# A block's down-projection by seven block products of eight, with the weight sums made by accumulating transfers

## The chip, the cores and the metric

The kernel runs on one core of a Trainium2 chip, in one launch. The metric is the device time of the execution in microseconds. Five engines work beside each other, each with its own queue in order: PE (TensorE), DVE (VectorE), ACT (ScalarE), POOL (GpSimd) and SP (SyncE, which here only issues transfers).

## What is computed

One decoder block for 2048 tokens of width 1024, in float32: a retention group and an attention group (8 heads each) side by side, an output projection, and a gated convolutional MLP. The change concerns the MLP, and the attention beside which it puts new work:

```python
def conv_ffn(h, w_up, conv_w, conv_b, w_down):
    S = h.shape[1]
    u = jnp.einsum('bsd,df->bsf', h, w_up)
    up = jnp.pad(u, ((0, 0), (CONV_WIDTH - 1, 0), (0, 0)))
    u = conv_b + sum(conv_w[j] * up[:, j:j + S] for j in range(CONV_WIDTH))
    gate, val = u[..., :D_FF], u[..., D_FF:]
    return jnp.einsum('bsf,fd->bsd', jax.nn.silu(gate) * val, w_down)
...
        x = x + conv_ffn(rms_norm(x, ffn_norm_w[l]), w_up[l], conv_w[l], conv_b[l], w_down[l])
    return rms_norm(x, final_norm_w)
```

D_FF is 2816, 22 blocks of 128.

## The kernel before

Every float32 product is made of three products of rounded parts: an operand is split into a high part (by ACT, L65) and the rest, called lo (by POOL or DVE, L69), and `mm3` (L71 to L75) multiplies high by high, high by lo and lo by high into one PSUM bank. So a split of 128x512 is one ACT and one POOL or DVE operation, and three matmuls of 128x128 by 128x512 make one block product.

The stages follow each other: the input projection to about 225 us; then retention (`ret_stream`) and attention (`att_stream`, L567), whose steps `side_by_side` (L482) mixes, and attention beside the first half of the output projection, to 1390 us; then for each half of 1024 tokens the forms of its tokens (`half_0_forms`, `half_1_forms`), the up-projection `up` (L1125) and the down-projection `down` (L1209). A scheduler sets the order of each engine from the order in which these streams issue their steps. In attention POOL adds up denominators (`den`, L793) from ACT's exponentials (`pc`, L782), and splits q and k as they are loaded; SP loads q, k, kpe and v (L718 to L734) and stores denominators (`den_s`, L807) and outputs in one queue.

`up` already multiplies 2x2 blocks with seven products in place of eight (Strassen-Winograd): per block fb of 128 features 7 x 12 matmuls. The sums of weight blocks that this needs are made by POOL in `weight_forms` (L1091): per fb four additions or subtractions (L1095, L1108) and seven lo splits, a step of it at each product (`next(prep)` in `product`, L1138). DVE adds the products into u (L1147), does the convolution (L1153, L1154, 128x1024, with ACT's L1152) and the gate (L1178, L1179); g goes to `g_s` in DRAM.

`down` goes through two quarters q of four token tiles, for each through 22 blocks fb; a step has 4 x 2 x 3 = 24 matmuls into eight banks, so that it needs all of PSUM from its first step. Its g split's lo is DVE's, the two weight splits' lo POOL's; the loads (512 KB of weights, 256 KB of g) go two steps ahead. At the end of a quarter come the residual (`finish`, L1220), squares (L1226), `rstd` and the scaling (L1228 to L1231), and the stores, which `pay` (L915) issues.

Of the kernel before, what the change touches and what calls it, by code (L numbers as in the profile page):

```python
# [29 lines left out]
NFB = DFF // P  # L30
EPS = 1e-6
# [23 lines left out]
class Block:  # L55
# [511 lines left out]
    def att_stream(self):  # L567
# [11 lines left out]
        self.at, mx, owed = 0, maxima(), 0.0  # L579
        for n, (h, g) in enumerate(groups):  # L580
# [412 lines left out]
    def half_0_forms(self):  # L993
# [10 lines left out]
        for i in range(4):  # L1004
# [3 lines left out]
            if i == 0:  # L1008
                self.up_load(0)
# [16 lines left out]
    def z1_load(self, n, r=None):  # L1026
        t = Z1_ORDER[n]
        r = (self.raws[n % 2] if r is None else r).rearrange("p (a k x) -> p a k x", a=2, k=4)
        self.att_load(t, r, self.p1.rearrange("p (k x) -> p k x", k=4), self.ms[n % 2].rearrange("p (a k x) -> p a k x", a=2, k=4))

    def z1_early(self, n):

        if n == 2 * NFB - 3:
            self.nc.sync.dma_start(self.u2.rearrange("p a b -> p (a b)"), self.a["ffn_norm_w"].broadcast_to([P, D]))
            self.ms = self.slots(1)
        if n >= 2 * NFB - 2:
            k = n - (2 * NFB - 2)
            self.z1_load(k, self.u.rearrange("p a b -> p (a b)")[:, k * D:(k + 1) * D])

    def half_1_forms(self):  # L1040
# [5 lines left out]
        for n, t in enumerate(Z1_ORDER):  # L1046
# [14 lines left out]
            if n == 1:  # L1061
                self.up_load(0)
# [19 lines left out]
    def all_forms(self, half):  # L1082
# [5 lines left out]
        for n in range(2):  # L1088
            yield from self.down_prepare(n)

    def weight_forms(self):  # L1091

        nc, a = self.nc, self.a
        t1, t2 = (self.fs[0][:, k * 512:(k + 1) * 512] for k in range(2))
        sub = lambda o, x, y: nc.gpsimd.tensor_tensor(o, x, y, op=ALU.subtract)  # L1095
        W = self.W = {}

        def raw(fb, j, k):
            return self.raws[(2 * fb + j + 2) % 4][:, k * 512:(k + 1) * 512]

        def put(fb, n, src):
            W[fb, n] = self.slot_split(src, P)
        for fb in range(NFB):
            self.up_load(fb + 1)
            g0, g1, v0, v1 = (raw(fb, j, k) for j in range(2) for k in range(2))
            put(fb, 0, g0)
            yield
            nc.gpsimd.tensor_tensor(t1, v0, v1, op=ALU.add)  # L1108
            sub(t2, t1, g0)
            put(fb, 1, t2)  # L1110
            yield
            sub(v0, g0, v0)
            put(fb, 6, v0)
            yield
            put(fb, 4, t1)
# [298 lines left out]
```

## Time and profile before

| what | value |
|---|---|
| median of 3 runs (lowest, highest) | 2917.74 us (2916.3, 2919.93) |
| the profiled execution's own time | 2915.82 us |
| its span, first to last instruction | 2914.0 us |
| mean granted TensorE clock | 0.976 of full speed |
| matmuls | 12672 |
| moved by the DMA engines | 332.85 MB, all issued by SP but 2.4 MB of instructions |

Busy times are those of one profiled execution. A line such as L69 can be a helper's, so groups are told apart by the tile that they write (w, F, k, den). "Idle before, <-releaser" is the time in which an engine stood still ahead of these instructions and what let it go on. A stretch gives each engine's busy time with the number of its instructions.

### The profile page before, as it was taken

The numbers are of one execution on the slowest core, as the hardware profiler recorded it, in microseconds if no ns is written. First come the engines' busy times: TensorE is split into PE (matmuls) and PEld (weight loads), VectorE is DVE, ScalarE is ACT, GpSimd is POOL, SyncE is SP. The second block draws the span as 40 slices with busy tenths as digits, with TensorE's granted clock in tenths as the row PEclk, the third lists the DMA queues.
The fourth block names the chain that finished last, engine by engine and source line by source line (L and its number), as shares of the span: only waits on it lengthen the run. The fifth ranks groups of instructions, "written<-read, shape, count | busy, mean of one in ns | idle before, by whom it ended". The sixth has DMA issues, their size and how long they took to land.

```text
span 2914.0 us, 37511 instructions
## 1 busy us (share of the span) xinstructions
PE 2726.3 (94%) x12672; PEld 2217.6 (76%) x12672; DVE 1932.9 (66%) x3349; ACT 1353.5 (46%) x2588; POOL 1976.0 (68%) x1480
## 2 busy tenths in 40 slices
PE   7998999998999999989999999899986999999998
PEld 6976777776777777767788887688874888887887
DVE  8756766767776776844468888834165888886243
ACT  5435566566665565651333343334334443333243
POOL 2035665666655565664699999776568999995564
PEclk9999999999999999989999999999997999999999
DMA  7663122222211121335722222375462222225453
GB/s 262 225 206 93 45 66 69 66 77 83 80 53 61 54 66 44 95 109 200 249 71 87 83 69 87 101 235 178 155 205 73 87 82 71 87 72 174 145 198 106
DMA packets 153506, 332.85 MB, mean 114 GB/s; under 512 B 35033, under 2 KB 68569, under 8 KB 147169
## 3 DMA queue, kind: packets, MB, share of 16 engines
q1 hardware_dynamic: 153312, 330.45, 35.3%
q8 instruction: 100, 1.64, 0.2%
q14 instruction: 94, 0.76, 0.1%
HBM read 237.64 MB, written 92.75 MB: 113 GB/s over the span
## 4 chain that ended last, share of the span: by engine, by line
PE 54%; DVE 3%; POOL 3%; DMA 2%; ACT 1%; issue 1%; SPq 0%; POOLq 0%; ACTq 0%; DVEq 0%
PE b L75 16%; PE b L74 16%; PE b L73 16%; DMA raw<-mixa_s 1%; PE x L677 1%; PE pm L74 1%; PE pm L75 1%; PE pm L73 1%; POOL w L69 1%; POOL F L69 0%; POOL m L69 0%; PE sm L743 0%; PE u L75 0%; PE s L775 0%; DVE w L1154 0%
## 5 line engine op out<-in xcount | busy, mean ns | idle before, releaser
L69 POOL TENSOR_TENSOR w<-raw,w 128x512 fp32r<-128x512 f32 (+2 forms) x315 | 519.7, 1667 | 243.5 <-ACT w L65 233.7
L74 PE MATMUL b<-F,w 128*128 128x512 f32 x1232 | 486.6, 395 | 6.6 <-POOL F L69 6.6
L75 PE MATMUL b<-F,w 128*128 128x512 f32 x1232 | 492.1, 399 | 0.0
L73 PE MATMUL b<-F,w 128*128 128x512 f32 x1232 | 485.3, 394 | 0.0
L793 POOL TENSOR_TENSOR den<-den,pc 128x512 f32<-128x512 f32 (+2 forms) x256 | 294.9, 1152 | 231.7 <-ACT pc L782 213.5
L65 ACT ACTIVATE w<-raw 128x512 fp32r<-128x512 f32 (+2 forms) x328 | 214.6, 658 | 336.6 <-PE b L75 191.6
L73 PE MATMUL b<-w 128*128 128x512 f32 x832 | 329.1, 396 | 19.6 <-DVE u L1147 11.3
L74 PE MATMUL b<-w 128*128 128x512 f32 x832 | 327.4, 393 | 0.0
L75 PE MATMUL b<-w 128*128 128x512 f32 x832 | 326.8, 393 | 0.0
L69 DVE TENSOR_TENSOR w<-xr,w 128x512 fp32r<-128x512 f32 x88 | 112.1, 1274 | 287.8 <-ACT w L65 287.8
L74 PEld LDWEIGHTS b<-F,w 128*128 128x128 f32 x1232 | 232.1, 188 | 66.9 <-POOL F L69 7.1
L73 PEld LDWEIGHTS b<-F,w 128*128 128x128 f32 x1232 | 232.1, 188 | 56.7 <-DVE u L1147 1.5
L75 PEld LDWEIGHTS b<-F,w 128*128 128x128 f32 x1232 | 232.0, 188 | 53.7
L784 DVE TENSOR_TENSOR pc<-s,pc 128x512 fp32r<-128x512 f32 (+1 forms) x320 | 197.2, 618 | 95.3 <-ACT s L783 74.8
L782 ACT ACTIVATE pc<-s 128x512 fp32r<-128x512 f32 (+1 forms) x320 | 173.2, 541 | 176.8 <-PE s L780 172.4
L1153 DVE SCALAR_TENSOR_TENSOR w<-u,cw,w 128x1024 f32<-128x1024 f32 x88 | 163.9, 1863 | 127.5 <-ACT w L1152 127.5
L1152 ACT ACTIVATE w<-u,cw 128x1024 f32<-128x1024 f32 x88 | 109.5, 1244 | 271.1 <-DVE u L1147 234.3
L73 PE MATMUL pm<-w,h 128*128 128x512 f32 x512 | 209.3, 409 | 11.4 <-DVE r_g L126 3.8
L74 PE MATMUL pm<-w,h 128*128 128x512 f32 x512 | 203.6, 398 | 0.0
L69 POOL TENSOR_TENSOR w<-xr,w 128x512 fp32r<-128x512 f32 x110 | 200.9, 1843 | 3.4 <-ACT w L65 3.4
L75 PE MATMUL pm<-w,h 128*128 128x512 f32 x512 | 203.1, 397 | 0.0
L73 PEld LDWEIGHTS b<-w 128*128 128x128 f32 x832 | 158.2, 190 | 56.5 <-DVE u L1147 15.0
(271 smaller groups left out, 6608.9 us busy)
## 6 DMA issues: line engine op xcount, KB each, us to landing
raw<-in_w_down SPq DMA_DIRECT2D x88, 512.0 KB
h<-hT_s SPq DMA_DIRECT2D x32, 1024.0 KB
xr<-in_w_up SPq DMA_DIRECT2D x44, 512.0 KB
raw<-in_w_up SPq DMA_DIRECT2D x44, 512.0 KB
g_s<-w SPq DMA_DIRECT2D x44, 512.0 KB
xr<-g_s SPq DMA_DIRECT2D x88, 256.0 KB
hT_s<-hT SPq DMA_DIRECT2D x16, 1024.0 KB
raw<-in_w_ret SPq DMA_DIRECT2D x16, 512.0 KB
```

The lines of the kernel that those rows point to most:

```text
L65: nc.scalar.activation(hi, src, AF.Copy)
L69: eng.tensor_tensor(lo, src, f32(hi), op=ALU.subtract)
L73: mm(out, lhsT=lh, rhs=rh, start=start, stop=False)
L74: mm(out, lhsT=lh, rhs=rl, start=False, stop=False)
L75: mm(out, lhsT=ll, rhs=rh, start=False, stop=stop)
L677: mm(ps[:, x * P:x * P + 256], lhsT=l, rhs=r, start=n == 0, stop=n == len(ops) - 1)
L782: nc.scalar.activation(pc[:, 0, r0:], ps[:, r0:], AF.Exp, scale=ATT_SCALE)
L784: nc.vector.tensor_tensor(pc[:, 1, r0:], ps[:, r0:], f32(pc[:, 0, r0:]), op=ALU.subtract)
L793: nc.gpsimd.tensor_tensor(den[:, r0:], den[:, r0:], hi[:, r0:], op=ALU.add)
L1152: nc.scalar.activation(acc, x[:, 2:1026], AF.Identity, scale=w2, bias=b)
L1153: nc.vector.scalar_tensor_tensor(acc, x[:, 1:1025], w1, acc, op0=ALU.mult, op1=ALU.add)
```

## The change

The down-projection of a half becomes one 2x2 block product with seven products: the token halves (512 tokens) and halves of the 2816 features on one side, the halves of features and of output columns on the other. Each product p has 11 blocks of 128 features, so there are 77 steps (`ND`), each with 4 x 3 = 12 matmuls into four banks, one per token tile. The g rows lie in a tile G (22 x 512 KB), loaded by `row(k)` in the steps listed; G takes the place of the up-projection's tile F. DVE makes the sums of the token side (`sums(i)`, 44 operations of 128x512 in steps 6 to 49) and adds each product to the four result blocks it belongs to (`meet`: for the first ACT makes four copies per token tile, for the other six DVE makes 1, 2, 2, 3, 1 and 1 additions per tile, 40 in all). A step's two splits have their lo on DVE (POOL for the first three). The closing of the rows is spread over the last steps; the half's last steps do one eviction, one square and a closing per tile.

The sums of weight blocks, four for the up-projection (22 blocks of 256 KB each) and four for the down-projection (11 blocks each), are made in DRAM during attention: one operand is copied by a DRAM-to-DRAM transfer from SP, and the other is added by an accumulating transfer from POOL. `att_stream` asks for one transfer at every third step of `att_group`, 60 copies and 60 accumulating ones in all (512 KB each for up, 768 or 512 KB for down). `weight_forms` then only loads the seven forms of an fb (1.79 MB in place of 1 MB) and splits them. The weights lie in DRAM in blocks that fit this. Some signs change in `up`.

```diff
@@ att_stream, after L586 @@
             for c in self.att_group(h, g, qs.pop(n)):
+                step += 1
+                if step % 3 == 0:
+                    next(sums, None)
...
+        for _ in sums:
+            pass
         self.finish()
...
+    def sums(self):
+
+        sy, po = self.nc.sync.dma_start, self.nc.gpsimd.dma_start
+        rows = lambda t: t.rearrange("b p f -> (b p f)").rearrange("(n x) -> n x", x=2048)
+        for stage in range(6):
+            for n, size, (w0, w1, w2, w3), (s1, s2, s3, s4) in self.summed:
+                for dst, src, add in (
+                        [(s1, w2, False), (s3, w2, False)], [(s1, w3, True), (s3, w0, True)],
+                        [(s2, s1, False)], [(s2, w0, True)], [(s4, s2, False)], [(s4, w1, True)])[stage]:
+                    for k in range(0, n, size):
+                        sl = slice(k, min(k + size, n))
+                        if add:
+                            po(rows(dst[sl]), rows(src[sl]), accum_op=ALU.add, max_dma_last_dim=2048)
+                        else:
+                            sy(rows(dst[sl]), rows(src[sl]))
+                        yield
...
-    def up_load(self, fb):
-        if fb < NFB:
-            for j in range(2):
-                self.nc.sync.dma_start(self.raws[(2 * fb + j + 2) % 4], self.a["w_up"][j * NFB + fb].rearrange("p k f -> p (k f)"))
+    def form_load(self, i):
+
+        if i < 7 * NFB:
+            fb, n = divmod(i, 7)
+            src = [self.a["w_up"][0], self.sum_s[1], self.sum_s[2], self.sum_s[0], self.a["w_up"][3], self.sum_s[3], self.a["w_up"][1]][n]
+            self.nc.sync.dma_start(self.form_raw(i), src[fb])
...
     def weight_forms(self):
...
-            nc.gpsimd.tensor_tensor(t1, v0, v1, op=ALU.add)
-            sub(t2, t1, g0)
...
-            sub(v0, g0, v0)
...
-            sub(g0, g1, t2)
...
+        for i in range(7 * NFB):
+            fb, n = divmod(i, 7)
+            W[fb, (0, 1, 6, 4, 2, 3, 5)[n]] = self.slot_split(self.form_raw(i), P)
+            self.form_load(i + 8)
             yield
...
     def up(self, half):
-            add(u2, product(fb, 1), p1)
-            add(u3, product(fb, 6), u2)
+            sub(u2, product(fb, 1), p1)
+            sub(u3, u2, product(fb, 6))
...
     def down_load(self, n):
+        if n < ND:
+            p, k = divmod(n, NKB)
+            src = [self.wd(0, 0), self.wd(1, 0), self.sumd_s[2], self.sumd_s[0], self.sumd_s[1], self.wd(1, 1), self.sumd_s[3]][p]
+            if n < 4:
+                self.nc.sync.dma_start(self.raws[n][:, 0:512], self.g_s[self.half, k][:, 0:512])
+            self.nc.sync.dma_start(self.down_raw(n), src[k])
...
     def down_prepare(self, n):
+            eng = "pool" if n < 3 else "dve"
...
+            g = self.slot_split(src, P, eng)
             yield
...
+            self.rows[n] = (g, self.slot_split(self.down_raw(n), 512, eng))
...
+            if n > 1:
+                for m in {2: (4, 5), 3: (6, 7, 8)}.get(n, (n + 5,)):
+                    self.down_load(m)
...
     def down(self, half, ctx):
+        G = self.G = yp.tile([P, NFB, D], F32, name="G")
...
         def block(n, t):
+            (gh, gl), (wh, wl) = self.rows[n]
+            self.mm3(banks[n // NKB][t], gh[:, t, :], gl[:, t, :], wh[:, 0, :], wl[:, 0, :], n % NKB == 0, n % NKB == NKB - 1)
...
+        def sums(i):
+
+            A = lambda row, half, k: G[:, row * NKB + k, half * 512:(half + 1) * 512]
+            p, k = divmod(i, NKB)
+            if p == 0:
+                k = (k + 4) % NKB
+                tt(self.s3[k], A(0, 0, k), A(0, 1, k), ALU.subtract)
...
+        def meet(p, t):
+
+            b = banks[p][t]
+            (c11, c12), (c21, c22) = C[t], C[4 + t]
+            if p == 0:
+                for c, sign in ((c11, 1.0), (c21, 1.0), (c22, -1.0), (c12, -1.0)):
+                    nc.scalar.activation(c, b, AF.Copy, scale=sign)
...
+        for n, ks in enumerate(((4, 5), (6,), (7,), (8,), (9,), (10,), (0,), (11,), (12, 1), (13,), (14, 2), (15,), (16, 3))):
+            for k in ks:
+                at(n, row, k)
+        for k in range(17, NFB):
+            at(k - 4, row, k)
+        for i in range(4 * NKB):
+            at(6 + i, sums, i)
+        for p in range(6):
+            for t in range(4):
+                at(NKB * p + 13 + t * (2 if p == 4 else 1), meet, p, t)
...
+        banks, last = {}, 4 if half else 0
+        for n in range(ND - last):
+            if n % NKB == 0:
+                banks[n // NKB] = [self.bank() for _ in range(4)]
             for t in range(4):
                 block(n, t)
+            prepare(n + 3)
+            for f, args in todo.pop(n, ()):
+                f(*args)
```

The scheduler's order, at three places. The first is SP's queue early in attention (in the trace of before the stretch from 254 to 272 us). There `sum_s` is a sum of up-projection weights (L616 a copy) and `den_s` the store of denominators (L833, before L807). Before:

```order
L734 DMA raw<-q_s 96x512
L718 DMA raw<-k_s 64x512
L837 DMA mixa_s<-ot 64x4x128
L832 DMA denl_s<-otl 1x512
L837 DMA mixa_s<-ot 64x4x128
L719 DMA raw<-kpe_s 34x512
L721 DMA raw<-v_s 128x4x64
L734 DMA raw<-q_s 96x512
L807 DMA den_s<-otl 1x512
L718 DMA raw<-k_s 64x512
```

Now:

```order
L616 DMA sum_s<-in_w_up 16x8192
L736 DMA mix_s<-m 128x2x128
L616 DMA sum_s<-in_w_up 16x8192
L833 DMA den_s<-otl 1x512
L760 DMA raw<-q_s 96x512
L616 DMA sum_s<-in_w_up 16x8192
L744 DMA raw<-k_s 64x512
L745 DMA raw<-kpe_s 34x512
L747 DMA raw<-v_s 128x4x64
L863 DMA mixa_s<-ot 64x4x128
L858 DMA denl_s<-otl 1x512
L616 DMA sum_s<-in_w_up 16x8192
```

Copies stand between the loads and stores, and the load of q that stood ahead of den_s now stands behind it.

The second is POOL's queue at about the same place; L614 is an accumulating transfer. Before, den additions (L793):

```order
L789 TENSOR_TENSOR den<-pc 128x512
L69 TENSOR_TENSOR v_2447<-raw,v_2447 128x4x64
L627 TENSOR_TENSOR vs<-vg,gam 128x128
L793 TENSOR_TENSOR den<-den,pc 128x512 x2
L69 TENSOR_TENSOR V<-vs,V 128x4x64
L793 TENSOR_TENSOR den<-den,pc 128x512
L69 TENSOR_TENSOR S<-qk,S 128x8x64
L793 TENSOR_TENSOR den<-den,pc 128x384
```

Now (L819 is the den addition, L653 the vs product):

```order
L819 TENSOR_TENSOR den<-den,pc 128x512
L614 DMA sum_s<-in_w_up 256x512
L819 TENSOR_TENSOR den<-den,pc 128x512
L614 DMA sum_s<-in_w_up 256x512
L819 TENSOR_TENSOR den<-den,pc 128x512
L73 TENSOR_TENSOR q<-raw,q 96x512
L819 TENSOR_TENSOR den<-den,pc 128x384
L653 TENSOR_TENSOR vs<-vg,gam 128x128
L819 TENSOR_TENSOR den<-den,pc 128x256
L614 DMA sum_s<-in_w_up 256x512
```

Between den additions POOL now issues accumulating transfers. Each of the early ones waits for the copy that SP issued last ahead of it. All 120 transfers stand ahead of the place that the kernel before reached at about 575 us.

The third is DVE inside the first half's down-projection. Before (w<-xr is the lo split of g):

```order
L69 TENSOR_TENSOR w<-xr_14772,w 128x512
L69 TENSOR_TENSOR w<-xr_14771,w 128x512
L69 TENSOR_TENSOR w<-xr_14772,w 128x512
L69 TENSOR_TENSOR w<-xr_14771,w 128x512
L69 TENSOR_TENSOR w<-xr_14772,w 128x512
```

Now, where the first product meets its results (w<-raw and w<-xr are lo splits of weights, w<-w those of token sums, G<-G a token sum, u<-b an addition of a product):

```order
L1262 TENSOR_TENSOR G<-G 128x512 x3
L73 TENSOR_TENSOR w<-w 128x512
L73 TENSOR_TENSOR w<-raw,w 128x512
L1262 TENSOR_TENSOR u<-b,u 128x512 x2
L73 TENSOR_TENSOR w<-w 128x512
L73 TENSOR_TENSOR w<-raw,w 128x512
L1262 TENSOR_TENSOR u<-b,u 128x512 x2
L73 TENSOR_TENSOR w<-w 128x512
L73 TENSOR_TENSOR w<-xr_14893,w 128x512
L1262 TENSOR_TENSOR G<-G 128x512 x3
L73 TENSOR_TENSOR w<-w 128x512
L73 TENSOR_TENSOR w<-xr_14893,w 128x512
```

Where DVE had one split per 24 matmuls it now has two per 12, and token sums and additions of products between them. On POOL, `weight_forms` has 154 splits per half and nothing else, where there were 242 operations.

## Rows read from the trace of the kernel before

**Rows 1.** The page, part 1: busy time, share and instructions.

```profile
PE 2726.3 (94%) x12672; PEld 2217.6 (76%) x12672; DVE 1932.9 (66%) x3349; ACT 1353.5 (46%) x2588; POOL 1976.0 (68%) x1480
```

**Rows 2.** Stretches: length, busy (count) of each engine, PE clock, DMA share, GB/s.

```profile
core 0: us, PE busy (x) PEld busy (x) DVE busy (x) ACT busy (x) POOL busy (x), PEclk, DMA share, GB/s
166.00:575.00 409.00, 372.16 (x1860) 296.91 (x1859) 278.60 (x644) 228.97 (x483) 232.67 (x240) 0.98 0.29 85
...
1449.50:1879.50 430.00, 430.00 (x1841) 344.90 (x1841) 339.65 (x274) 167.75 (x258) 414.16 (x238) 1.00 0.26 82
1879.50:1902.00 22.50, 13.57 (x35) 8.83 (x34) 19.43 (x17) 8.78 (x15) 11.49 (x7) 0.62 0.56 189
1902.00:2133.00 231.00, 231.00 (x1021) 191.27 (x1020) 74.68 (x97) 82.89 (x156) 143.73 (x100) 1.00 0.57 184
2133.00:2236.00 103.00, 64.59 (x285) 52.83 (x284) 67.48 (x170) 43.37 (x84) 80.82 (x60) 0.80 0.47 160
2661.50:2670.00 8.50, 6.09 (x25) 4.38 (x24) 6.96 (x9) 2.92 (x4) 5.00 (x3) 0.97 0.61 217
2670.00:2905.00 235.00, 235.00 (x1033) 194.39 (x1032) 86.91 (x128) 83.43 (x157) 129.59 (x87) 0.99 0.50 164
```

**Rows 3.** Timeline of PE, first change from up to down: start, length, [idle <-releaser].

```profile
1883.26 0.50 PE L73 MATMUL b<-w 128*128 128x512 f32 x1 [2.18 <-DVE u L1147]
...
1889.55 0.80 PE L73 MATMUL b<-w 128*128 128x512 f32 x1 [5.32 <-DVE u L1147]
1890.14 0.63 PE L74 MATMUL b<-w 128*128 128x512 f32 x1
```

**Rows 4.** Timeline of all engines from PE's last matmul.

```profile
2905.18 1.37 DVE L1220 TENSOR_TENSOR y<-b,y 128x512 f32<-128x512 f32 x2 [0.21 <-PE b L75]
...
2905.43 0.39 PE L75 MATMUL b<-w 128*128 128x512 f32 x1
...
2906.72 0.63 ACT L1226 ACTIVATE sq<-y 128x512 f32<-128x512 f32 x1
```

**Rows 5.** Groups of POOL in the first up-projection: busy, mean ns | idle <-releaser.

```profile
L69 POOL TENSOR_TENSOR w<-raw,w 128x512 fp32r<-128x512 f32 x59 | 106.4, 1816 | 11.4 <-ACT w L65 8.4 <-PE b L75 3.0
...
L1108 POOL TENSOR_TENSOR w<-raw 128x512 f32<-128x512 f32 x11 | 22.9, 2078 | 0.9
```

**Rows 6.** Waits while the second half's forms are made: us, times, longest.

```profile
PE b L971 <- DVE w L1058: 23.6, 3, 12.5
...
PEld b L74 <- POOL F L69: 7.1, 1, 7.1
```

**Rows 7.** Groups: DVE by form, whole span; ACT in the first down-projection.

```profile
L1147 DVE TENSOR_TENSOR u<-b,u 128x512 f32<-128x512 f32 x220 | 142.9, 682 | 10.4 <-PE b L75 6.0
...
L65 ACT ACTIVATE w<-raw 128x512 fp32r<-128x512 f32 x80 | 49.5, 623 | 117.1 <-PE b L75 79.9 <-DMA raw<-in_w_down 22.8 <-issue 8.0
```

**Rows 8.** One tile, w on DVE: ns min/median/max, first and last start.

```profile
L69 DVE TENSOR_TENSOR w<-xr,w x88: 673/1370/1785, 1867.2 to 2884.7; 128x512 fp32r<-128x512 f32 x88
```

**Rows 9.** Timelines of DVE and of POOL in the first down-projection.

```profile
1913.88 0.69 DVE L69 TENSOR_TENSOR w<-xr,w 128x512 fp32r<-128x512 f32 x1 [4.13 <-ACT w L65]
...
1914.45 1.29 POOL L69 TENSOR_TENSOR w<-raw,w 128x512 fp32r<-128x512 f32 x1 [1.46 <-ACT w L65]
```

**Rows 10.** Waits in the attention stretch: us, times, longest.

```profile
POOL den L793 <- ACT pc L782: 64.2, 45, 6.1
...
ACT k L65 <- DMA raw<-kpe_s: 11.7, 7, 3.1
```

**Rows 11.** Timelines of SP's queue and of ACT at 250 to 271 us.

```profile
254.55 0.31 SPq L734 DMA_DIRECT2D raw<-q_s  x1
...
270.69 0.22 SPq L807 DMA_DIRECT2D den_s<-otl  x1
...
260.68 0.62 ACT L65 ACTIVATE q<-raw 96x512 fp32r<-96x512 f32 x1
```

**Rows 12.** SP's issues of one line: ns min/median/max.

```profile
L541 SPq DMA_DIRECT2D h<-hT_s x32: 320/349/602, 185.0 to 1187.7; - x32
```

More of the change, by code (lines that the diff above doesn't have):

```diff
@@ L578, in maxima @@
                 done.add(n)
-        self.at, mx, owed = 0, maxima(), 0.0
+        self.at, mx, owed, sums, step = 0, maxima(), 0.0, self.sums(), 0
         for n, (h, g) in enumerate(groups):
@@ L1191, in down_begin @@
         self.turn_ = self.turn_ % len(self.order)
-        self.down_load(0)
-        self.down_load(1)
+        for n in range(4):
+            self.down_load(n)
+        self.s3 = [f[:, j * 512:(j + 1) * 512] for f in self.fs for j in range(2)] + [self.u2[:, 0], self.u2[:, 1], self.p1]
     def down_prepare(self, n):
-        if n < 2 * NFB:
-            if n == 2 * NFB - 6 and self.half == 0:
+        if n < ND:
+            p, k = divmod(n, NKB)
+            if n == ND - 8 and self.half == 0:
@@ L1200, in down_prepare @@
                 self.order, self.turn_ = self.order[6:], 0
-            w = self.raws[n % 2]
-            r = self.rows[n] = [self.slot_split(self.raws[2 + n % 2][:, 0:512], P, "dve")]
-            yield
-            for dh in range(2):
-                r.append(self.slot_split(w[:, dh * 512:(dh + 1) * 512], 512))
-                yield
-            self.down_load(n + 2)
+            eng = "pool" if n < 3 else "dve"
+            if n < 4:
+                src = self.raws[n][:, 0:512]
+            elif p == 2:
+                src = self.s3[k]
+            else:
+                row, half = [(0, 0), (1, 0), None, (0, 1), (0, 0), (1, 0), (1, 1)][p]
+                src = self.G[:, row * NKB + k, half * 512:(half + 1) * 512]
@@ new lines, in residual, with square, early @@
+        def residual(t, dh, place, add):
+            if add:
+                tt(C[t][dh], C[t][dh], place, ALU.add)
+            else:
+                nc.sync.dma_start(place, self.y_s[t0 + t][:, dh * 512:(dh + 1) * 512])
+        def square(t, dh):
+            nc.scalar.activation(scratch[t % 2], C[t][dh], AF.Square, scale=D ** -0.5, accum_out=ss[:, t, dh:dh + 1])
+        def early(t, dh):
+            square(t, dh)
+            nc.gpsimd.tensor_tensor(C[t][dh], C[t][dh], onw[:, dh], op=ALU.mult)
@@ new lines, in close, with at @@
+        def close(t, dh):
+            e, l = C[t][1 - dh], C[t][dh]
+            square(t, dh)
+            r = self.rstd(self.cs, ss[:, t, 0:1], "n", more=ss[:, t, 1:2])
+            nc.scalar.activation(e, e, AF.Copy, scale=r)
+            nc.vector.scalar_tensor_tensor(l, l, r, onw[:, dh], op0=ALU.mult, op1=ALU.mult)
+            for j in range(2):
+                self.owed.append((a["out"][(t0 + t) * P:(t0 + t + 1) * P, j * 512:(j + 1) * 512], C[t][j]))
+        todo = {}
+        def at(n, f, *args):
+            todo.setdefault(n, []).append((f, args))
@@ new lines, in down @@
+        at(43, nc.sync.dma_start, onw, a["final_norm_w"].broadcast_to([P, D]).rearrange("p (h f) -> p h f", h=2))
+        for t in range(4):
+            for dh in range(2):
+                j = 2 * t + dh
+                at(44 + t, residual, 4 + t, dh, G[:, j, 512:], False)
+                at(50 + j, residual, 4 + t, dh, G[:, j, 512:], True)
+                at(53 + t, residual, t, dh, G[:, j, 0:512], False)
+                at(64 + j, residual, t, dh, G[:, j, 0:512], True)
+            at(66 + t, early, 4 + t, 1)
+            at(67 + 2 * t if t < 3 else 72, early, t, 0)
+            at(72 + t, close, t, 1)
@@ new lines, in down @@
+        banks, last = {}, 4 if half else 0
+        for n in range(ND - last):
+            if n % NKB == 0:
+                banks[n // NKB] = [self.bank() for _ in range(4)]
+            for t in range(4):
+                block(n, t)
+            prepare(n + 3)
+            for f, args in todo.pop(n, ()):
+                f(*args)
+        if last:
+            prepare(ND - 1)
+        for n in sorted(todo):
+            for f, args in todo[n]:
+                f(*args)
+        if half:
+            self.pay()
@@ L1283, in run @@
+        for t in range(4):
+            for n in range(ND - last, ND):
+                block(n, t)
+            meet(6, t)
+            close(4 + t, 0)
+            if half:
+                self.pay()
     def run(self):
```

155 lines of the change are left out of this document (59 added, 96 removed).

## The prediction

> **What bounds the kernel now.** I read the page's first part and then the stretches. TensorE (PE) is busy for 94% of the span [rows 1], so an average can hide no second bound of this size; what matters is where PE is not busy. The table of stretches shows three kinds. In the up-projection (430.00 of 430.00 us) and in the down-projection (231.00 of 231.00, 235.00 of 235.00) PE never pauses [rows 2]: there only fewer matmuls help. Between up and down, and while the second half's forms are made (64.59 of 103.00), it pauses for other engines. In the attention stretch that the weight sums go into, 166 to 575 us, PE is busy 372.16 of 409.00, DVE 278.60, ACT 228.97, POOL 232.67, and the DMA engines only 0.29 of the time [rows 2].
>
> **Part 1, fewer matmuls.** A half of the down-projection has 44 steps of 24 matmuls, 1056; it gets 77 steps of 12, 924. Both halves together lose 264. In the stretches in which PE does nothing else 1021 of them took 231.00 us and 1033 took 235.00, 0.226 and 0.227 us each [rows 2], the same rate in both halves. 264 x 0.227 = **-59.9 us**, as far as PE stays the bound; a few missing records would make each matmul a little shorter, never longer.
>
> **Part 2, whether PE stays the bound in the new down-projection.** A half should take 924 x 0.227 = 210 us. DVE gets, per half: 148 lo splits (two per step, the first three steps' being POOL's), 44 token sums, 40 additions of products, 16 of the residual: 248 operations of 128x512. With a PSUM operand such an addition takes 682 ns [rows 7]. With both operands in SBUF it took 673 to 1785 ns, median 1370 [rows 8], and the row at 1913.88 us shows why: 0.69 us in a moment in which POOL stood still (its next operation, at 1914.45, had 1.46 us of idle time ahead of it) [rows 9]. In the new down-projection POOL has hardly any work left: three preparations, eight multiplications, four weight rows. So I take 0.69 us: 171 us, and some 21 us for eight closings (nine small operations of about 0.2 us and one of 0.75), 192 of 210. It fits, with little left. ACT's 154 hi splits at 623 ns [rows 7] are 96 us, and some 20 for copies and squares: covered. The loads: 17 rows of g at 512 KB and 22 weight blocks of 256 KB in the first 17 steps (46 us) are 14.7 MB, 319 GB/s. The densest stretch in the table, 8.5 us at the second half's transition, moved 217 GB/s at a share of 0.61, which is 356 at a full share [rows 2]; and each row is asked for some ten steps (27 us) before its use. Cost: between 0 and 30 us (a tenth of DVE's work late); I take **+5**, near the lower end because the steps are prepared three ahead.
>
> **Part 3, the weight sums leave POOL.** In the up-projection POOL has per block four sums and seven lo splits, 11 operations of 1.8 to 2.1 us [rows 5], and was busy 414 of 430 us [rows 2]: it paces, and it stretches DVE's two-input operations beside it. DVE ends late: at the change to down PE waits 2.18 and 5.32 us for DVE's u, and a matmul then takes 0.80 and 0.63 us [rows 3], at a granted clock of 0.62 in that stretch [rows 2]. The stretch 1879.50 to 1902 had 35 matmuls, worth 7.9 us, in 22.5, a loss of 14.6; that of the second half 25 in 8.5, a loss of 2.8 [rows 2]. With seven operations POOL needs some 13 of 19.6 us per block, DVE's run shorter, and the first product needs four banks, not eight. Bounds 0 and -17; I take **-12**, most of it, as DVE's last chain itself (two 1024-wide passes per gate) stays. The up-projection proper gains nothing, since PE was never idle there. Its loads grow from 1 to 1.79 MB per block, 91 GB/s instead of 53, on DMA engines used 0.26 [rows 2]: nothing. In the second half's forms POOL no longer does sums ahead of F's lo split, for which PE's weight loads wait 7.1 us; the 23.6 us for L1058 are DVE's, partly stretched by POOL [rows 6]. Bounds 0 and -15, taken **-5**.
>
> **Part 4, the end.** After the last matmul (2905.43) there were two evictions and two squares in a row [rows 4]; now one of each is left. Half of the 1.37 us of the evictions and 0.63 of a square: **-1.3**.
>
> **Part 5, the sums in attention.** New are 60 copies on SP and 60 accumulating transfers on POOL, of 512 or 768 KB each, 34.6 MB copied and 34.6 MB accumulated. The order puts them all into what was 166 to 575 us. The trace has no transfer issued by POOL, no accumulating one and none from DRAM to DRAM; so bounds. Below: an issue costs SP 0.32 to 0.60 us [rows 12]; 60 of these on POOL are 21 us, and POOL has 176 us idle: 0. A gain could come from the changed order alone, as no work there is taken away; I exclude it. Above: POOL stands still for a copy's whole trip. 1 MB read and written, at 250 GB/s (an estimate between the 217 and 356 above), is 4.2 us, and 60 x 4.2 = 252, 76 more than the idle time: **+76**. Beside this, SP's order changes: the load of q that SP issued at 254.55 now stands behind the store den_s, which could go only at 270.69, and ACT wanted its q at 260.68 [rows 11]. That is 10 us late at one place, unless the consumer moves too. What a late load costs is in the waits: ACT's k waited 11.7 us on seven loads, 1.7 each [rows 10]. If one transfer in ten makes such a wait reach PE, 12 x 1.7 = **+20**. I take that, nearer to the lower end, since POOL already waits 64.2 us there for ACT's pc [rows 10], which an issue can fill.
>
> In that stretch DVE is busy 278.60 of 409.00 us [rows 2], so an issue on POOL will often meet a DVE operation. The Trainium skill speaks against part 5 here: "SBUF — State Buffer", section "SBUF: two separate sides", says that the descriptors of a GpSimd-issued transfer can't be written while DVE runs a two-port operation, and its part on the bandwidth-pool intuition gives 0.62 us for such a transfer alone and 3.1 us beside one. By the first figure the 60 issues would be 37 us and hidden, by the second 186, an estimate, 10 over POOL's idle time: part 5 would be 0 by the one and 10 by the other. No row here shows either.
>
> **Sum.** The profiled execution took 2915.8 us, 1.9 below the runs' median of 2917.7. 2915.8 - 59.9 + 5 - 12 - 5 - 1.3 + 20 = 2862.6; against the median, 1.9 higher, **2864 us** (rounded down).
>
> **Rivals.** A: the sums cost nothing. For it: DMA share 0.29, POOL idle 43% of the stretch. Against: the moved q load. 2864 - 20 = 2844; with all of part 3 down to 2832.
>
> B, slower: POOL's queue is held by the accumulating transfers. Each of the early ones waits, in POOL's order, for the copy just issued on SP, which itself stands behind stores that wait for ACT; behind it in POOL stand the den additions, and PE's scores wait for the buffers that these free. It decides from 176 / 60 = 2.9 us of POOL per transfer; past that each microsecond costs 60. At 4.5 us it costs 96 in place of 20: 2940. It is slower than before from about 4.2 us. For it: the waits in the order, 4.2 us for a copy. Against: SP often has a store's wait to spare, and later accumulates follow older copies.
>
> C: DVE bounds the new down-projection. It decides where its mean operation passes (210 - 21) / 248 = 0.76 us; at 0.85, a fourth of the way to the median beside POOL [rows 8], a half takes 232 us, 22 longer: 2864 - 5 + 44 = 2903.
>
> D: DVE's lag at the change to down is its own and stays: 2864 + 12 = 2876, within the forecast's own range.
>
> **How the numbers follow.** Forecast, with D (2846 to 2890): 0.56. A: 0.12. C: 0.16, an eighth of it past 2912. B: 0.12. Between B and the forecast, 2912 to 2924: 0.04. 0.2%, 6 us, is about what a measurement of this kernel can tell from no change. Faster 0.56 + 0.12 + 0.14 = 0.82; same 0.02 + 0.04 = 0.06; slower 0.12. The range of 2832 to 2912 leaves out about 0.02 below and 0.18 above, and takes in part 5 up to some +65.
>
> **What would show it.** Right: matmuls of the two down-projections 264 fewer at 0.227 us with PE full in them; DVE at about 0.69 us an addition there; POOL's L69 operations in up below 1.8 us and its busy time down by a third; PE's loss at the first change to down under 6 us; the stretch of attention about 20 us longer. Wrong: PE pauses in down that DVE ends (C), POOL waits on a DMA ahead of den or the attention stretch over 80 us longer (B), or PE's loss at the changes as before (D).

## The result, and the profile after

The changed kernel takes 2884.31 us (median of 4, 2882.95 to 2886.74) against 2918.84 us before: 0.9887 of the time, 95% interval 0.9875 to 0.9900. It is 34.5 us faster; 54 had been forecast, and the range of 2832 to 2912 holds it. Errors in both directions stand behind the difference. In the profiled executions the first up-projection starts at 1505.6 us where it started at 1447.4, so the stages up to there lost 58 us and not 20; everything behind it gained 90 us, where the forecast had 73.

The page of the changed kernel, part 1 and two lines of part 3 (the queues: packets, MB, share of 16 engines):

```profile
PE 2676.8 (93%) x12408; PEld 2180.8 (76%) x12408; DVE 2054.8 (71%) x3725; ACT 1420.5 (49%) x2664; POOL 1397.8 (48%) x1200
...
q1 hardware_dynamic: 196096, 396.01, 42.6%
q0 software_dynamic: 17856, 34.61, 7.1%
```

POOL is down from 1976.0 us to 1397.8, and a second queue, POOL's own, has appeared with the 34.61 MB of the accumulating transfers; DVE has 122 us more [rows 1]. The stretches of the changed kernel, columns as in [rows 2]:

```profile
230.00:300.00 70.00, 51.29 (x199) 37.92 (x199) 43.86 (x92) 31.94 (x69) 37.99 (x39) 0.76 0.63 157
300.00:400.00 100.00, 94.79 (x486) 77.16 (x484) 67.59 (x155) 58.12 (x125) 75.82 (x79) 0.98 0.99 249
400.00:500.00 100.00, 81.22 (x390) 65.31 (x391) 63.91 (x143) 52.72 (x110) 63.44 (x67) 0.88 0.92 234
500.00:640.00 140.00, 115.85 (x590) 94.80 (x589) 83.75 (x202) 72.21 (x155) 90.01 (x98) 0.91 0.94 228
1505.60:1936.00 430.40, 430.40 (x1846) 346.27 (x1845) 316.32 (x286) 187.39 (x266) 234.73 (x158) 1.00 0.42 127
1936.00:1952.00 16.00, 16.00 (x72) 13.16 (x71) 14.73 (x21) 9.34 (x14) 0.00 (x0) 1.00 0.85 299
1952.00:2168.00 216.00, 216.00 (x955) 178.85 (x954) 182.86 (x335) 109.00 (x206) 44.69 (x31) 1.00 0.60 201
2168.00:2229.70 61.70, 34.98 (x161) 28.79 (x160) 44.71 (x98) 29.08 (x53) 43.91 (x33) 0.77 0.59 192
2672.00:2872.00 200.00, 200.00 (x884) 165.55 (x883) 165.83 (x301) 99.65 (x190) 12.05 (x8) 1.00 0.50 167
```

From 300 to 640 us the DMA engines are now busy 0.92 to 0.99 of the time, where the attention stretch had 0.29 [rows 2]. PE's busy share and granted clock fall together in two places: before 300 us, with the DMA engines at 0.63 (51.29 of 70 us at 0.76), and after 400 (81.22 of 100 us at 0.88). At the changes from up to down PE does not pause at all (16.00 of 16.00 us at the first, 10.00 of 10.00 at the second, from 2662 us), where 14.6 and 2.8 us were lost [rows 2, 3]; in the new down-projections it does not pause either (955 matmuls in 216.00 us, 884 in 200.00).

What the waits between 166 and 630 us say (engine, line, what it waited for: us, times, longest):

```profile
ACT k L69 <- DMA raw<-kpe_s: 35.6, 5, 13.4
...
POOL sum_s L614 <- DMA sum_s<-sum_s: 5.1, 4, 1.9
```

ACT's k waits 35.6 us for loads, 13.4 us once, where it was 11.7 in all [rows 10]. POOL's accumulating transfers wait only 7.3 us for copies, 5.1 of them on the line shown. One late load of k, from the timelines of SP, ACT and PE:

```profile
502.87 3.19 SPq L616 DMA_DIRECT2D sumd_s<-sumd_s  x4
506.15 2.83 SPq L616 DMA_DIRECT2D sum_s<-sum_s  x4
533.08 0.36 SPq L736 DMA_DIRECT2D mix_s<-m  x1
...
538.84 0.42 SPq L745 DMA_DIRECT2D raw<-kpe_s  x1
...
556.32 0.63 ACT L69 ACTIVATE k<-raw 98x512 fp32r<-98x512 f32 x1 [13.44 <-DMA raw<-kpe_s]
...
565.10 1.01 PE L830 MATMUL sm<-pc,ones 128*2 128x512 f32 x2 [16.11 <-DVE z_g L124]
```

SP issues eight copies from 502.87 to 509, then waits for a store until 533; k, asked for at 538.84, reaches ACT at 556.32, 17 us later, while the bytes of the sums are under way. ACT's work for retention stands behind k in its queue (th, L724, at 557.81), DVE's `z_g` behind that, and PE stood still for it for 16.11 us. And at the place of [rows 11]:

```profile
272.77 0.24 SPq L833 DMA_DIRECT2D den_s<-otl  x1
273.05 0.33 SPq L760 DMA_DIRECT2D raw<-q_s  x1
```

The load of q stands behind den_s as the order had it, and goes at 273.05, not 254.55. But between 166 and 630 us no engine shows a wait for a load of q: its consumer moved too, as the prediction allowed for.

### The profile page after: what moved, and what is told of

The parts are those of the page before. It is cut to its first block, busy times and chain, and to the rows that moved or that the text cites. A ratio compares the mean times of both kernels' runs of the same rounds, so it can differ in the third digit from the quotient of the medians.

```text
span 2882.7 us, 38021 instructions
## 1 busy us (share of the span) xinstructions
PE 2676.8 (93%) x12408; PEld 2180.8 (76%) x12408; DVE 2054.8 (71%) x3725; ACT 1420.5 (49%) x2664; POOL 1397.8 (48%) x1200
## 3 DMA queue, kind: packets, MB, share of 16 engines
q0 software_dynamic: 17856, 34.61, 7.1%
## 4 chain that ended last, share of the span: by engine, by line
PE 53%; DVE 3%; DMA 2%; POOL 2%; issue 1%; ACT 1%; SPq 0%; POOLq 0%; DVEq 0%; ACTq 0%
PE b L78 15%; PE b L79 15%; PE b L77 15%; DMA raw<-mixa_s 1%; PE x L703 1%; PE pm L79 1%; PE pm L78 1%; PE pm L77 1%; POOL m L73 0%; PE sm L769 0%; PE u L79 0%; PE b L997 0%; PE s L801 0%; PE o L825 0%; PE u L78 0%
## 5 line engine op out<-in xcount | busy, mean ns | idle before, releaser
L819 POOL TENSOR_TENSOR den<-den,pc 128x512 f32<-128x512 f32 (+2 forms) x256 | 301.9, 1179 | 205.7 <-ACT pc L808 189.0
L73 POOL TENSOR_TENSOR w<-raw,w 128x512 fp32r<-128x512 f32 (+2 forms) x189 | 291.2, 1547 | 224.4 <-ACT w L69 224.2
L73 POOL TENSOR_TENSOR w<-xr,w 128x512 fp32r<-128x512 f32 x160 | 238.0, 1494 | 203.1 <-ACT w L69 203.0
L69 ACT ACTIVATE w<-raw 128x512 fp32r<-128x512 f32 (+2 forms) x274 | 183.5, 672 | 241.0 <-PE b L78 169.1
L77 PE MATMUL b<-w 128*128 128x512 f32 x744 | 292.0, 393 | 9.0 <-DVE w L910 9.0
L78 PE MATMUL b<-w 128*128 128x512 f32 x744 | 291.0, 391 | 0.0
L79 PE MATMUL b<-w 128*128 128x512 f32 x744 | 290.8, 391 | 0.0
L69 ACT ACTIVATE w<-xr 128x512 fp32r<-128x512 f32 x238 | 148.5, 626 | 197.9 <-PE b L78 153.1
L77 PE MATMUL pm<-w,h 128*128 128x512 f32 x512 | 211.3, 413 | 22.3 <-ACT pc L808 7.6
L78 PE MATMUL pm<-w,h 128*128 128x512 f32 x512 | 206.1, 403 | 0.0
L79 PE MATMUL pm<-w,h 128*128 128x512 f32 x512 | 205.5, 401 | 0.0
L1167 DVE SCALAR_TENSOR_TENSOR w<-u,cw,w 128x1024 f32<-128x1024 f32 x88 | 116.1, 1320 | 114.5 <-ACT w L1166 114.5
L773 DVE TENSOR_REDUCE mx<-sm 128x1 f32<-128x512 f32 x192 | 131.9, 687 | 73.0 <-PE sm L769 71.9
L1168 DVE SCALAR_TENSOR_TENSOR w<-u,cw,w 128x1024 f32<-128x1024 f32 x88 | 182.0, 2068 | 1.6
```

The costliest lines, as they stand in the source:

```text
L69: nc.scalar.activation(hi, src, AF.Copy)
L73: eng.tensor_tensor(lo, src, f32(hi), op=ALU.subtract)
L77: mm(out, lhsT=lh, rhs=rh, start=start, stop=False)
L78: mm(out, lhsT=lh, rhs=rl, start=False, stop=False)
L79: mm(out, lhsT=ll, rhs=rh, start=False, stop=stop)
L773: nc.vector.tensor_reduce(mx[:, i, c:c + 1], ps[:, :w], axis=AX, op=ALU.max)
```

## Experiments

Twelve runs, each beside the kernel before on the same chip. "Up starts" is PE's first matmul of the first up-projection in the profiled execution.

| run | median us | ratio to before, 95% | up starts |
|---|---|---|---|
| changed kernel | 2884.3 | 0.9875 to 0.9900 | 1505.6 |
| e1_small | 2858.1 | 0.9780 to 0.9809 | 1481.3 |
| e2_copies | 2853.2 | 0.9768 to 0.9800 | 1473.2 |
| e3_adds | 2871.6 | 0.9830 to 0.9860 | 1496.9 |
| e4_none | 2831.9 | 0.9694 to 0.9723 | 1457.8 |
| e5_copies_small | 2844.1 | 0.9728 to 0.9764 | 1470.4 |
| e6_spread | 2876.9 | 0.9836 to 0.9881 | 1501.1 |
| e7_pool11 | 2888.3 | 0.9880 to 0.9924 | 1502.5 |
| e8_down_pool | 2908.6 | 0.9946 to 0.9978 | 1502.8 |
| e9_banks8 | 2884.9 | 0.9865 to 0.9913 | 1500.5 |
| e10_up_sums_back | 2863.8 | 0.9798 to 0.9827 | 1447.3 |
| e11_banks8_pool11 | 2893.2 | 0.9899 to 0.9927 | 1502.1 |
| e12_down_sums_early | 2861.3 | 0.9785 to 0.9840 | 1477.5 |

### What the sums cost in attention: e1 to e5

e1 cuts every transfer of the sums to its first row; e2 does so for the accumulating ones alone, e3 for the copies alone. The order of all other instructions up to the up-projection is that of the changed kernel. In e1 to e5 the forms are loaded from original weight blocks of the same size (those lines are left out here), so the sums are missing from the result.

```diff
-                            po(rows(dst[sl]), rows(src[sl]), accum_op=ALU.add, max_dma_last_dim=2048)
+                            po(rows(dst[sl])[0:1], rows(src[sl])[0:1], accum_op=ALU.add, max_dma_last_dim=2048)
...
-                            sy(rows(dst[sl]), rows(src[sl]))
+                            sy(rows(dst[sl])[0:1], rows(src[sl])[0:1])
```

> The changed kernel with all 120 transfers of the weight sums in their places in the same order on every engine, each with the same waits, but moving only its first 8 KB; the forms of the up- and down-projection are then read from original weight blocks of the same size (so the sums are left out of the result). In the changed kernel the up-projection starts 58 us later than before. Theory T (the bytes: loads of q, k and v stand behind the sums' bytes in the DMA engines, which are busy 0.9 to 1.05 of the time): nearly all comes back, the time is 2826 to 2834 us and the up-projection starts at 1446 to 1454. Rival Q (POOL's queue is held by the 60 issues and their waits for copies): issues stay, so at most the waits come back, 2870 to 2884. Rival O (the changed order of loads and stores): nothing comes back, 2880 to 2886.

> As e1, but the 60 copies keep their full size (34.6 MB) and only the accumulating transfers move 8 KB each. T by bytes alone: half of the 69 MB is gone, so at least half comes back, 2835 to 2855 us; if a saturated stretch alone costs, more than half. Q: 2870 to 2884. O: 2880 to 2886.

> As e1, but the 60 accumulating transfers keep their full size (34.6 MB) and only the copies move 8 KB each. T by bytes alone: the same as e2, 2835 to 2855 us. If accumulating transfers weigh more on the DMA engines than copies (each reads its destination too, and their queue's share was 7.1% of the span for 34.6 MB), later than e2 by 5 to 15. Q: 2870 to 2884. O: 2880 to 2886.

e4 leaves all 120 out (`sums` loops over nothing), and e5 the accumulating ones, with copies of one row (60 of them in its trace).

> The changed kernel without the 120 transfers; the order of the queues in attention is then again that of the kernel before, and the forms are read from original weight blocks (the sums are left out). All theories: the attention part as before, so 2884 - 54 to 58 = 2826 to 2830 us. What e1 takes more than this is the price of order and issues together: below 5 us by T, 40 to 55 by Q or O.

> As e1 with the accumulating transfers left out altogether: 58 copies of 8 KB on SP, nothing issued by POOL; the forms come from original blocks (sums left out). The scheduler still shifts the loads and stores of SP behind each other around the copies. e1 cost 26 us over the kernel without any of the transfers (e4, 2832 us). Theory Q' (POOL's 60 issues of 0.8 us and more fill its queue, and DVE's two-input operations are held while POOL runs without a gap: 5.64 us for one of 0.4 in e1): without issues most of the 26 comes back, 2832 to 2842 us, and no DVE addition of 128x256 takes over 3 us. Rival O (the order that the copies cause on SP and PE): 2850 to 2860.

The whole price is 2884.3 - 2831.9 = 52.4 us. e1 divides it in half: 26.2 us stay with 8 KB in each transfer, and 26.2 are the bytes. Neither T nor the two rivals alone had that. The bytes are no matter of their number either: copies at full size cost nothing over e1 (-4.9, about what such runs scatter), the accumulating ones 13.5, both together 26.2. e3 lies 18 us behind e2, more than the 5 to 15 expected. The rows of 400 to 500 us tell why (e1, e2 and e3 in this order, columns as in [rows 2], share and GB/s last):

```profile
400.00:500.00 100.00, 89.11 (x443) 71.92 (x444) 74.08 (x159) 55.03 (x115) 68.65 (x75) 0.97 0.23 63
```

```profile
400.00:500.00 100.00, 93.04 (x470) 75.74 (x469) 74.29 (x164) 56.99 (x119) 70.28 (x75) 0.98 0.55 183
```

```profile
400.00:500.00 100.00, 84.75 (x415) 68.67 (x414) 65.54 (x148) 56.62 (x118) 67.33 (x72) 0.91 0.76 150
```

With the same 34.6 MB the accumulating transfers hold the DMA engines 0.76 of the time, the copies 0.55; with both the changed kernel stands at 0.92 there. ACT's waits for loads of k between 166 and 630 us go the same way: 2.4 us in e1, 3.4 in e2, 22.6 in e3 and 35.6 in the changed kernel. Whether the accumulating itself or the size of the pieces makes the difference was not tested: the accumulating transfers went in 17856 packets of some 2 KB, the copies in larger ones.

The other half: e5 has no transfer on POOL and 12.2 us of it, so the order that the copies bring to SP and PE costs about 12 (rival O's part of it; e5 lies between the ranges of Q' and O). The largest part is lost between 235 and 265 us. SP's queue, then the stretch, of e4:

```profile
226.68 0.38 SPq L545 DMA_DIRECT2D h<-hT_s  x1
```

```profile
235.00:265.00 30.00, 24.54 (x117) 19.51 (x117) 17.54 (x43) 15.27 (x33) 17.53 (x19) 0.89 0.33 101
```

The same of e5, whose line 617 is a copy:

```profile
222.21 0.54 SPq L617 DMA_DIRECT2D sum_s<-in_w_up  x1
...
245.71 0.43 SPq L545 DMA_DIRECT2D h<-hT_s  x1
```

```profile
235.00:265.00 30.00, 23.13 (x81) 18.21 (x82) 14.98 (x43) 12.73 (x29) 12.72 (x13) 0.58 0.33 107
```

Where e4 loads h, the input of retention, e5's queue has copies, and h comes 19 us later. In both PE stands still for 6.0 us (for POOL's S) shortly before 240 us and the granted clock is 0.50 after it (1.2 GHz, the lower of its two levels). Then e4's PE has matmuls on h, without a pause, and is back at full clock by 245; e5's PE has none of them from 230 to 258 us, takes short attention steps with pauses between, and gets 81 matmuls done where e4 gets 117. All of this is before e5's q load, at 273.89. e1, e2, e3, e12 and the changed kernel, with copies at the same places, do 72 to 86 matmuls there at 0.56 to 0.68; the kernel before and e10, without them, 122 and 117 at 0.89.

The remaining 14 (e1 less e5) come with the accumulating transfers: the 60 issues, of 0.73 to 1.46 us each in e1, and what their places change. One mechanism in it the trace shows outright. Timelines of the changed kernel (its issues take 0.83 to 1.64 us), DVE, then POOL, then PE:

```profile
284.65 5.73 DVE L642 TENSOR_TENSOR qk<-t,t 128x256 f32<-128x256 f32 x1
```

```profile
282.12 1.01 POOL L819 TENSOR_TENSOR den<-den,pc 128x384 f32<-128x384 f32 x1
...
284.11 0.89 POOL L614 DMA_DIRECT2D sum_s<-in_w_up  x1
284.71 1.04 POOL L819 TENSOR_TENSOR den<-den,pc 128x256 f32<-128x256 f32 x1
...
289.09 1.00 POOL L73 TENSOR_TENSOR v<-raw,v 128x256 fp32r<-128x256 f32 x1
291.56 0.89 POOL L614 DMA_DIRECT2D sum_s<-in_w_up  x1 [1.47 <-DMA sum_s<-in_w_up]
```

```profile
291.71 1.01 PE L782 MATMUL sm<-ident,n 128*2 128x128 f32 x4 [4.70 <-DVE n L73]
```

All additions of that line (ns min/median/max):

```profile
L642 DVE TENSOR_TENSOR qk<-t,t x64: 412/568/5733, 199.3 to 1310.4; 128x256 f32<-128x256 f32 x64
```

From 282.12 to 290.09 POOL had no pause, the issue at 284.11 standing in it, and DVE's addition, 0.57 us in the median, stood for 5.73; it ended when POOL paused. Before, the longest of this line took 1.95. PE waited 4.70 us for DVE's chain behind it. e1 to e3 have this at the same place (5.63 to 5.72 us); e4 has no operation of DVE of that shape over 3 us. e5 has two of 4.1, on another line, without any issue on POOL, so an issue is not needed for it. This one place is some 20 of the 70 matmuls by which e1's PE falls behind e5's between 280 and 640 us; where the rest of the 14 us goes was not found.

### Spreading them: e6

```diff
+                            if self.gate is not None:
+                                sy(rows(dst[sl])[0:1, 0:512], self.gate)
                             sy(rows(dst[sl]), rows(src[sl]))
...
         self.finish = finish
+        self.gate = self.denl_s[g, h].rearrange("i p -> (i p)").unsqueeze(0)
```

> The changed kernel with each copy held back until the attention group before it has stored its denominators (a 2 KB transfer from that store into the copy's first row, which the copy then overwrites), so that the sums spread over all of attention, 166 to about 1390 us, at the rate at which the program asks for them, and not by where the scheduler finds room. All sums are made. Theory: the bytes then come at 69 MB in 1200 us, 58 GB/s more, a DMA share near 0.5, so that most of the 26 us that the bytes cost (changed kernel less e1) comes back; of the other 26 a part, as POOL's issues stand wider apart: 2845 to 2865 us. Rival O: order and issues cost the same wherever they stand, and the gates add 60 transfers to SP: 2860 to 2880. If the price is by transfer and not by density: 2880 to 2890.

A miss: 2876.9 us, 7 less than the changed kernel and far from the 2845 to 2865 of the theory. The engines are at half load now (e6, 1000 to 1200 us):

```profile
1000.00:1200.00 200.00, 178.92 (x895) 144.26 (x894) 137.22 (x302) 111.66 (x234) 122.65 (x126) 0.95 0.56 143
```

Yet PE loses time again and again up to 1200 us, where the changed kernel lost next to nothing between 627 us, its last transfer, and 1300. So density alone is not the price; rival O's 2860 to 2880 held the result. The spread was not even (a DMA share of 0.77 from 300 to 500 us, 0.28 to 640), and the 58 gates on SP are a part of this price that was not measured by itself; which places cost what stays open.

### Why the waits at the change to down went away: e7, e9, e11

e7 gives POOL four additions per block back; e9 takes eight banks in step 0 again; e11 does both. In e7 and e11 the additions overwrite rows that the second half's forms use (e7's expectation takes them for a tile that nothing reads), so these forms are lost.

```diff
             W[fb, (0, 1, 6, 4, 2, 3, 5)[n]] = self.slot_split(self.form_raw(i), P)
+            if n < 4:
+                self.nc.gpsimd.tensor_tensor(self.fs[0][:, 0:512], self.form_raw(i), self.form_raw(i), op=ALU.add)
```

```diff
+            if n == 0:
+                banks[1] = [self.bank() for _ in range(4)]
             for t in range(4):
                 block(n, t)
+                if n == 0:
+                    (gh, gl), (wh, wl) = self.rows[n]
+                    self.mm3(banks[1][t], gh[:, t, :], gl[:, t, :], wh[:, 0, :], wl[:, 0, :], True, True)
```

> The changed kernel with four additions of 128x512 put back on POOL for each block of the up-projection, 11 operations as before (they write a tile that nothing reads). Theory of part 3 (POOL's load in up makes DVE late at the change to down): the losses at the changes come back, 10 to 17 us, 2894 to 2902 us, and PE waits for DVE's u after the first products of down. Rival D turned round (the four banks in place of eight remove the wait by themselves): 2884 to 2888, no wait of PE there.

> The changed kernel whose down-projection touches eight banks in its first step again: the second product's four banks are taken in step 0 and written by one block product each (12 matmuls per half that the second product's start overwrites; 24 x 0.227 = 5.4 us of extra work). e7 showed that POOL's eleven operations do not bring the wait at the change back. Theory (the four banks removed it: PE no longer wants the bank that DVE still reads): PE waits for DVE's u again in step 0, 2 to 8 us per half, 2884 + 5 + 4 to 16 = 2893 to 2905 us. Rival (DVE's chain is shorter because POOL is lighter, so eight banks are free in time too): 2888 to 2892, no wait for u.

> e9 and e7 together: eight banks in the first step and POOL's four additions per block back (they overwrite rows that the second half's forms still read, so those are not computed). If the wait at the change came from POOL and banks together, as the kernel before had both: 10 to 17 us over e7 (2888) and 5 for the extra matmuls, 2903 to 2910. If from the banks alone: as e9 and 4 more. If from neither: 2893.

No run of the three brought the wait back, as e7's and e9's rivals had it: none has a pause of PE over 0.6 us at either change. With eleven operations POOL is busy 371 of 428 us in e7, not the 414 of 430 of before [rows 2]:

```profile
1508.00:1936.00 428.00, 428.00 (x1836) 344.34 (x1835) 334.27 (x285) 173.20 (x263) 371.34 (x237) 1.00 0.43 126
```

So neither the banks nor these additions are the cause alone. e10 and e12 below, with before's real sums on POOL and the new down, need 236.1 and 237.4 us for the 1020 matmuls from the first change on that the changed kernel does in 231.0: 5 to 6 us lost there, none at the second change. Of the 17.4 us, then, some 11 to 12 went with the new down-projection's start and 5 to 6 with POOL's sums. Which part of the new start it is (three steps prepared, their splits on POOL, other loads) stays open.

### Whether DVE had room in the new down: e8

```diff
-            self.rows[n] = (g, self.slot_split(self.down_raw(n), 512, eng))
+            self.rows[n] = (g, self.slot_split(self.down_raw(n), 512, "pool"))
```

> The changed kernel with the weights' lo splits of the down-projection on POOL in place of DVE, as in the kernel before. DVE then has 171 operations of 128x512 per half, not 248, but POOL beside it in 77 x 1.3 to 1.8 us of 210. By part 2's price PE stays the bound while DVE's mean operation is under (210 - 21) / 171 = 1.10 us: with 131 of them stretched to at most 1.37 and 40 at 0.68 the mean is at most 1.21, 18 us late per half. Expected: 2884 to 2896 us, DVE's additions with two SBUF inputs at 0.9 to 1.3 us. Rival (DVE is the bound already, and lightening it helps): below 2880.

24 us slower than the changed kernel, above what was expected. Groups of DVE in its first down-projection (busy, mean ns | idle) and waits (us, times, longest), and then the same groups of the changed kernel:

```profile
L73 DVE TENSOR_TENSOR w<-G,w 128x512 fp32r<-128x512 f32 x62 | 67.5, 1101 | 36.1 <-ACT w L69 29.5 <-PE b L78 6.6
...
L1262 DVE TENSOR_TENSOR w<-G 128x512 f32<-128x512 f32 x8 | 10.9, 1370 | 0.0
```

```profile
PEld b L78 <- POOL w L73: 8.3, 5, 3.6
PEld b L79 <- DVE w L73: 6.6, 4, 3.8
```

```profile
L73 DVE TENSOR_TENSOR w<-G,w 128x512 fp32r<-128x512 f32 x62 | 45.5, 735 | 20.8 <-ACT w L69 20.7
...
L1262 DVE TENSOR_TENSOR G<-G 128x512 f32<-128x512 f32 x33 | 21.5, 685 | 0.1
...
L1262 DVE TENSOR_TENSOR w<-G 128x512 f32<-128x512 f32 x8 | 5.3, 684 | 0.0
```

With POOL at work beside it, DVE's splits take 1101 ns, not 735, and sums into w 1370, not 684, at two thirds of the operations; PE waits for POOL's splits and for DVE's. How much of the 24 us is DVE's and how much POOL's own splits, the runs do not part; but the new down runs as it does because POOL has little to do beside it.

### A faster kernel: e10 and e12

Both put the up-projection's sums back on POOL and keep the new down. e12 asks for the 32 transfers of the down-projection's sums in attention, e10 in the first up-projection, held back by g blocks:

```diff
+        sums = self.sums() if half == 0 else iter(())
         for fb in range(NFB):
+            if fb > 1:
+                self.gate = self.g_s[half, fb - 2][0:1, 0:512]
+                for _ in range(2):
+                    next(sums, None)
```

> The up-projection's weight sums are made by POOL again (loads, operations and signs as in the kernel before), the down-projection stays new, and its 16 copies and 16 accumulating transfers are made during the first up-projection, each copy held back until the g block of two blocks before is stored. Attention then has no transfer of sums, and its order is that of the kernel without any (e4, 2832 us). Theory (the price of the change lay in attention; POOL's eleven operations in up cost 4 us, e7, and its sums ahead of F's lo split in the second half's forms some 7): 2836 to 2850 us. Rival 1 (POOL, busy 415 of 430 us with its sums, has no room for 16 issues of 0.95 us, and up grows by as much): 2850 to 2865. Rival 2 (accumulating transfers delay the loads of up or down as they did in attention): above 2865, with PE idle in up.

> As e10, but the 32 transfers are asked for in attention, as the changed kernel does; the scheduler puts them all early, into SP's queue where the changed kernel has its first ones. By the number of transfers, 32 of 120 of 52 us are 14: 14 over e10. Theory (order, issues and bytes each cost at the place where they stand, and the first 10 us of the changed kernel's loss came within the first 25 transfers): 10 to 25 over e10. Rival (DMA density alone): below 5 over e10, as 18 MB spread over 200 us do not fill the engines.

e10 takes 2863.8 us, 0.9798 to 0.9827 of before, 20 us less than the changed kernel. Its attention costs nothing (up starts at 1447.3), but its up-projection grew to 452.3 us, by 20: rival 1's size, with part of rival 2. Two of its waits from 1460 to 1930 us, and the stretch of this up-projection:

```profile
PEld b L77 <- DVE u L1168: 20.4, 8, 7.3
...
ACT w L1176 <- DMA g_s<-w: 15.3, 3, 6.5
```

```profile
1447.30:1899.50 452.20, 437.42 (x1848) 349.46 (x1847) 348.92 (x273) 169.82 (x260) 426.01 (x259) 0.98 0.48 132
```

ACT waits 15.3 us for the stores of g, which SP issues in one queue with the copies, and POOL, at 426 of 452 us, is full. e12, 2861.3 us, comes to the same by another way: up is 431.7 us again, and in its profiled execution (2874.7 us, the slowest of its four) some 24 us are lost between 227 and 323 us. Its theory, 10 to 25 us over e10, missed. That the two totals are alike, as e12's rival had it, comes from e10's loss in up and not from density.

## Why the prediction was right, and where not

The time fell inside the range partly by luck: part 5 and the loads of the forms cost some 40 us more than the sum had, and parts 2 and 3 gave some 17 more than it had.

Part 1 held: PE does 884 matmuls in 200.00 us, 0.226 each, in the new down as in the old.

Part 2 held, its +5 was not needed. DVE's operations of 128x512 took 676 to 686 ns in most groups, 735 to 864 in the splits and one group of additions, 0.72 us in the mean of the first down-projection (expected 0.69; rival C's limit was 0.76), and PE never paused. The DMA engines stood at 0.85 and 299 GB/s at the start (319 were needed by the estimate). Rival C did not come, by a small distance, and e8 shows its mechanism at work as soon as POOL is not idle.

Part 3 had the right size and the wrong cause. At the changes 17.4 us were won, the upper bound, not 12. "POOL paces, and it stretches DVE" was named first; with four additions back on POOL (e7) all of this gain stayed, and with its real sums (e10, e12) two thirds. Rival D, that DVE's lag stays, fell. The second half's forms and the start of its up-projection won 11 us, not 5: the wait of 7.1 us for F's lo split is gone; one of 7.0 is there again in e10 and one of 6.7 in e12, so there the reason given was the right one. But the forms' loads, which this part put at nothing, cost some 8 us ahead of the first up-projection. e4, which has no transfer of sums, starts it 10 us later than before (2.4 of them are there by 225 us): after its wait for the normed rows `hn_s` its PE goes on at 1404.50 us, at 1394.10 before, and at 1393.92 in e10, which loads the up weights as before.

Part 4 failed, though small: -1.3 forecast, +2.1 came. The end of the changed kernel, DVE and ACT:

```profile
2873.18 0.68 DVE L1262 TENSOR_TENSOR R<-b,R 128x512 f32<-128x512 f32 x1
...
2873.95 0.63 ACT L1307 ACTIVATE G<-R 128x512 f32<-128x512 f32 x1 [1.35 <-DVE R L1262]
...
2875.51 0.75 DVE L1318 SCALAR_TENSOR_TENSOR R<-R,r_n,G 128x512 f32<-128x512 f32 x1
...
2878.30 0.75 DVE L1318 SCALAR_TENSOR_TENSOR R<-R,r_n,G 128x512 f32<-128x512 f32 x1
```

Eviction and square are one each, but three closings now run through DVE's chains of small operations one after another, and the last starts late: PE ends at 2872, the last scaling starts at 2878.30.

Part 5 is the step that failed: +20 forecast, +52 measured (against e4), inside the bounds of 0 and 76 and far above the choice. "One transfer in ten makes such a wait reach PE", at 1.7 us, missed both halves. The waits for k became 7.1 us each, not 1.7, with the DMA engines near full: by the prediction's own figures 69 MB in 409 us are 169 GB/s beside 85, of some 356 at a full share, and it made no term of that. The order cost 12 by itself, and not through the q load that was named, for which nothing waits, but for the most part through the load of h and the clock behind it. The third share, 14, came with POOL's issues, which the prediction took to fill idle time. Rival B, POOL standing for whole copies, did not come: POOL waited 7.3 us for them, and an issue took about 0.9 us of POOL, neither 0.62 nor 3.1. The rule of the Trainium skill weighed there ("SBUF — State Buffer", "SBUF: two separate sides") did not decide: the longest of the 60 issues took 1.64 us. What came is a wait the other way round, DVE held while POOL worked.

## What to carry to other kernels

Work that looks free because its engines are idle half the time is paid in the queues that it is put into: here half the price was the order and the issues, with 8 KB in each transfer, and spreading the transfers took only 7 of the 52 us off. A queue with new work in it also puts off what stood there: look first at the loads that moved. Test that with the bytes cut to nothing in unchanged order before looking at bandwidth. And before moving work off an engine, look at what it costs where it is: POOL's sums for the up-projection cost some 12 us there (5 to 6 at the change, 7 in the forms), and a kernel that keeps them (e10) is 20 us faster than the changed one.

## What was not expected of the hardware

An addition of 128x256 on DVE was held for 5.73 us, until POOL paused, where its median is 0.57; the Trainium skill ("SBUF — State Buffer", section "SBUF: two separate sides") calls the port that both use an exclusive lock. The rows agree in that DVE stood still while POOL worked; but it stood through five of POOL's operations, one after another, and that it was this port that held it no run here shows. DRAM-to-DRAM copies and accumulating transfers of the same 34.6 MB held the DMA engines very differently from 400 to 500 us, 0.55 and 0.76 of the time (0.23 with neither, in e1).
